# A Hyena and neighbourhood-attention layer: the order of the two tiles of each convolution product

## The chip, the cores and the metric

The kernel runs on one core of a Trainium2 chip. A core has a matrix engine (TensorE, PE in the profile; its weight loads are listed as PEld), a vector engine (VectorE, DVE), a scalar engine (ScalarE, ACT), a general engine (GpSimd, POOL) and a queue that only issues transfers here (SyncE, SP). Each works through its own list of instructions in order; semaphores make one wait for another. Matrix products go to PSUM, eight banks of 128 x 512 float32, and are copied from there to SBUF. The metric is the device time of one execution in microseconds; lower is better.

## The reference

One layer for two groups of tokens that share weights: 128 context tokens and 512 latent tokens, 640 columns together, 1024 channels. The input is modulated and projected; one branch is a gated long convolution, the other an attention; both are gated, projected, merged and normalised. What matters here is the convolution branch:

```python
hy, g_h, qkv, g_a, m = split(z)                      # z = h @ w_in
hy = short_conv(hy, conv_w, conv_b)                  # three taps along the sequence
v_h, x1, x0 = jnp.split(hy, 3, axis=-1)
...
u = v_h * x1
uf = jnp.fft.rfft(u, n=2 * L, axis=1)
ff = jnp.fft.rfft(filt_full, n=2 * L, axis=0)
y = jnp.fft.irfft(uf * ff, n=2 * L, axis=1)[:, :L]
y_h = (y + u * d_bias) * x0
...
p_h = (y_h * silu(g_h)) @ w_bh
```

So each channel of `u` is a product of two projected and three-tap-filtered values, `v_h` and `x1`. The order in which the two are made has no part in the result.

## The kernel before

Channels lie on the 128 partitions, tokens on the free axis (640 columns; 641 with a gap column between the two groups). A weight tile `wall[i]` gives 128 output channels. `proj(i)` (the loop of `accumulate`, L168) multiplies it in float32 split into a high and a low part: three passes (high x high, high x low, low x high) for each of 8 blocks of the inner dimension, in two halves of 320 columns, so 48 matmuls for each tile, into two PSUM banks of the pool `mm` (four banks, so two tiles). The split of the weights is made by ScalarE and VectorE (`split`, L101, L102), or, in the convolution part, by ScalarE (`wl` L147, `wh` L149) and an accumulating transfer that POOL issues (L148). `wh` has two buffers, `wl` three; the raw weights are loaded by SP (L63).

`conv_tile(i, dst)` runs `proj(i)`, copies the banks with four ScalarE instructions (L468 to L472) into one of two staging tiles `zs` in turn, and makes the three taps into `dst`: one on ScalarE (L474), two on VectorE (L476). Both `zs` and `dst` have to be free for that.

The 1024 channels of the convolution are done in four quarters of two tiles each, with these stages:

- `quarter_head(q)`: for each of the quarter's two tiles n the tile `u` (from `v_h`, weight tile n) and the tile `x1` (weight tile 8 + n), then `u = u * x1` (L499). `u` comes from a pool of four buffers (tag "u", each one row of tokens for 128 channels), so the tile of quarter q + 2 takes the buffer of quarter q; `x1` from a pool of two (tag "cv"), which `x0` shares.
- `long_conv(q)` and `long_conv_back(q)`: transposes (L531), the transform by matrix products (L156 to L158), the product with the filter's spectrum, the transform back (yb), transposes back (yp L616, y L626); then `u` takes the result in place (L619, L628) and is multiplied into the gated row `yh` (`gapped_product`, L457, L461), which goes to memory (L508). With that the buffer of `u` is free.
- `filter_spectrum(q)`: the spectrum of the filter, from small matmuls (fl, fa, fb, fc, fd, fp).
- `quarter_tail(q)`: `x0` (weight tile 16 + n) and the gate (24 + n, L481, L486), multiplied into `yh`.

The first quarter's head runs with its filter; then for q = 0, 1, 2 one generator chains the head of q + 1 and the tail of q, and another the transform of q and its way back with the filter of q + 1; `weave` interleaves the two by steps. That is the order in which the instructions are written. The order in which they stand on the engines is chosen by a scheduler that plays them through with a cost model and takes from each engine's candidates what is ready; PSUM banks and buffers are dealt out as it goes. A change of the written order so moves other instructions too. The fourth quarter's transform runs with the first steps of the attention. When it is done, the memory of the convolution is released to the attention's tiles: POOL clears the mask tiles (L792), the mask is loaded, and keys are copied out (`k_half`, L712, L717).

After the attention, a merge stage multiplies the rows `yh` by `w_bh` (L168, L481), with the gate's rows added on VectorE (L1189), then the attention's rows by `w_ba`; an output projection and the normalisation end the kernel.

Of the kernel before, what the change touches and what calls it, by code (L numbers as in the profile page):

```python
# [45 lines left out]
def tile_hyena_natten_step(ctx: ExitStack, tc: tile.TileContext, a, o):  # L46
# [126 lines left out]
    def proj(i, xh=None, xl=None, eng=None):  # L173
        if i in banks:
            return banks.pop(i)
        w = wtile(i, eng)
        ps = bank(i)
        for k in range(NK):
            accumulate(ps, w, k, xh[k] if xh else hH[:, k], xl[k] if xl else hL[:, k])
            if k < NK - 1:  # L180
                yield
        return ps
# [267 lines left out]
    def by_row(t):  # L450
        return t.rearrange("p (r b c) -> p r b c", r=8, b=8)

    def from_blocks(t, n):
        return t.rearrange("p (b r c) -> p r b c", b=n, r=8)
# [8 lines left out]
    def conv_tile(i, dst):  # L463
        lo, hi = yield from proj(i, eng="dma")
        convw = out["convw"]
        zs = zss[0]
        zss.reverse()
        nc.scalar.activation(zs[:, 1 : 1 + LP], lo[:, :LP], AF.Copy)  # L468
        nat = by_row(zs[:, GAP + 1 : NG + 1])
        nc.scalar.activation(nat[:, :, 7:8], from_blocks(lo[:, B7], 1), AF.Copy)  # L470
        nc.scalar.activation(nat[:, :, 0:2], from_blocks(lo[:, B01], 2), AF.Copy)  # L471
        nc.scalar.activation(nat[:, :, 2:7], from_blocks(hi[:, :HALF], 5), AF.Copy)  # L472
        d = dst[:, :NG]
        nc.scalar.activation(d, zs[:, 1 : 1 + NG], AF.Identity, scale=convw[:, i, 1:2], bias=convw[:, i, 3:4])  # L474
        for c in (0, 2):
            nc.vector.scalar_tensor_tensor(d, zs[:, c : c + NG], convw[:, i, c : c + 1], d, op0=ALU.mult, op1=ALU.add)  # L476
# [12 lines left out]
    def quarter_head(q):  # L489
        us = []  # L490
        out[f"u{q}"] = us
        for i in range(2):
            n = 2 * q + i
            u = hw.tile([P, NG + 1], F32, tag="u", bufs=4, name=f"u{n}")
            x1 = hwa.tile([P, NG + 1], F32, tag="cv", bufs=2, name=f"x1_{n}")
            yield from conv_tile(n, u)
            yield
            yield from conv_tile(8 + n, x1)
            nc.vector.tensor_tensor(u[:, :NG], u[:, :NG], x1[:, :NG], op=ALU.mult)  # L499
            us.append(u)  # L500
            yield
# [147 lines left out]
    with tc.manual_schedule(engines={mybir.EngineType.PE, mybir.EngineType.DVE, mybir.EngineType.Activation}):  # L649
        prologue()  # L650
    tc.keep_in_program_order(last[0])
    head = quarter_head(0)
    next(head)
    dft_consts()
    weave(head, filter_spectrum(0), 2 + NK, N_FILTER)
    pinned[0] = False
    for q in range(3):
        weave(chain(quarter_head(q + 1), quarter_tail(q)), chain(long_conv(q), braid(long_conv_back(q), filter_spectrum(q + 1))),
              8 * NK, N_CONV + N_BACK + N_FILTER)
# [799 lines left out]
```

## Time and profile before

| | |
|---|---|
| median of 3 runs | 905.71 us (902.41 to 907.54) |
| profiled execution | 906.42 us, span 904.4 us, mean granted clock 0.993 |
| PE, PEld busy | 881.4 us (97%), 850.8 us (94%) |
| DVE, ACT, POOL busy | 625.2 us (69%), 423.9 us (47%), 162.4 us (18%) |
| moved by transfers | 124.43 MB, mean 138 GB/s |

A line of the profile names the source line (L168), the engine, the operation, and the tiles as output <- input with buffer numbers left out; so all `conv_tile` products are `mm`. "x672" counts instructions. Behind a bar or in brackets stands the idle time of the engine just before, with what ended it. In a table by stretches, each row gives the stretch, its length, then busy time and number of instructions of PE, PEld, DVE, ACT and POOL, the granted clock of TensorE as a share of full speed, the share of the transfer engines and GB/s. A list of waits gives the total in us, how often, and the longest.

Times of instructions of a kind overlap: a matmul's listed length (about 0.31 us for 320 columns) is longer than the distance from one start to the next, so distances are what counts for TensorE.

### The profile page before, as it was taken

The numbers are of one execution on the slowest core, as the hardware profiler recorded it, in microseconds if no ns is written. First come the engines' busy times: TensorE is split into PE (matmuls) and PEld (weight loads), VectorE is DVE, ScalarE is ACT, GpSimd is POOL, SyncE is SP. The second block draws the span as 40 slices with busy tenths as digits, with TensorE's granted clock in tenths as the row PEclk, the third lists the DMA queues.
The fourth block names the chain that finished last, engine by engine and source line by source line (L and its number), as shares of the span: only waits on it lengthen the run. The fifth ranks groups of instructions, "written<-read, shape, count | busy, mean of one in ns | idle before, by whom it ended". The sixth has DMA issues, their size and how long they took to land. (4 is left out here: it accounts for less than half of the span.)

```text
span 904.4 us, 16943 instructions
## 1 busy us (share of the span) xinstructions
PE 881.4 (97%) x6560; PEld 850.8 (94%) x6560; DVE 625.2 (69%) x1229; ACT 423.9 (47%) x909; POOL 162.4 (18%) x188
## 2 busy tenths in 40 slices
PE   8999999999999999999999999899999999999994
PEld 7899999999999999999999999899999989999883
DVE  4776784794777678488867578756767567567665
ACT  4395455645455333265566455545655532233200
POOL 0011010101001000086653322332332000000000
PEclk9999999999999999999999999999999999999997
DMA  8965655665646222323233322332343677445322
GB/s 310 400 166 135 137 133 119 153 127 127 154 101 151 75 62 92 108 83 88 78 110 119 117 80 90 113 120 89 119 132 100 187 279 234 168 163 181 121 96 87
DMA packets 56715, 124.43 MB, mean 138 GB/s; under 512 B 8603, under 2 KB 28059, under 8 KB 56636
## 3 DMA queue, kind: packets, MB, share of 16 engines
q1 hardware_dynamic: 46988, 103.07, 35.2%
q0 software_dynamic: 4032, 14.68, 10.0%
q10 hardware_dynamic: 5616, 5.61, 1.8%
q8 instruction: 52, 0.85, 0.4%
q14 instruction: 27, 0.22, 0.1%
HBM read 109.18 MB, written 14.16 MB: 136 GB/s over the span
## 5 line engine op out<-in xcount | busy, mean ns | idle before, releaser
L168 PE MATMUL mm<-hH,wh 128*128 128x320 f32 x672 | 160.1, 312 | 1.8 <-ACT zs L471 1.0
L168 PE MATMUL mm<-hH,wl 128*128 128x320 f32 x672 | 158.4, 310 | 0.4 <-DVE wl L102 0.4
L168 PE MATMUL mm<-hL,wh 128*128 128x320 f32 x672 | 158.6, 311 | 0.0
L168 PEld LDWEIGHTS mm<-hH,wh 128*128 128x128 f32 x672 | 112.9, 188 | 4.7 <-issue 1.8
L168 PEld LDWEIGHTS mm<-hH,wl 128*128 128x128 f32 x672 | 113.5, 188 | 1.3 <-DVE wl L102 0.9
L168 PEld LDWEIGHTS mm<-hL,wh 128*128 128x128 f32 x672 | 113.3, 188 | 1.1 <-DVE hL L315 0.5
L1054 PE MATMUL sp<-t,wb 128*128 128x320 f32 x672 | 105.4, 310 | 0.0
L1054 PEld LDWEIGHTS sp<-t,wb 128*128 128x128 f32 x672 | 99.5, 188 | 0.3 <-issue 0.3
L1054 PE MATMUL sp<-hH,wb 128*128 128x320 f32 x336 | 82.1, 314 | 0.5 <-DVE c L1069 0.5
L101 ACT ACTIVATE wh<-raw 128x1024 fp32r<-128x1024 f32 x38 | 40.2, 1061 | 70.3 <-PE mm L168 40.3
L148 POOL DMA_DIRECT2D wl<-wall x28 | 24.4, 871 | 262.6 <-ACT wl L147 225.0
L102 DVE TENSOR_TENSOR wl<-raw,wh 128x1024 fp32r<-128x1024 f32 x38 | 47.2, 1245 | 26.1 <-ACT wh L101 25.9
L1054 PEld LDWEIGHTS sp<-hH,wb 128*128 128x128 f32 x336 | 57.9, 188 | 2.8 <-issue 1.7
L149 ACT ACTIVATE wh<-raw 128x1024 fp32r<-128x1024 f32 x28 | 29.7, 1060 | 52.7 <-PE mm L168 52.6
L101 ACT ACTIVATE wb<-s 128x512 fp32r<-128x512 f32 x56 | 34.8, 628 | 41.8 <-DVE s L1027 28.7
L102 DVE TENSOR_TENSOR wb<-s,wb 128x512 fp32r<-128x512 f32 x56 | 39.1, 705 | 19.9 <-ACT wb L101 19.6
L1054 PE MATMUL sp<-hL,wb 128*128 128x320 f32 x168 | 51.8, 309 | 0.0
L168 PE MATMUL mm<-yhs,wh 128*128 128x320 f32 x256 | 49.6, 314 | 1.5 <-DVE mh L481 1.5
L840 POOL TENSOR_SCALAR p<-p,sm 128x384 f32<-128x384 f32 x32 | 45.1, 1421 | 25.2 <-DVE sm L839 13.9
L1283 PE MATMUL out<-woh,yhs 128*128 128x512 f32 (+1 forms) x176 | 45.6, 373 | 0.0
L168 PEld LDWEIGHTS mm<-yhs,wh 128*128 128x128 f32 x256 | 41.3, 192 | 1.8 <-issue 1.7
L840 POOL TENSOR_SCALAR edge<-edge,sm 128x320 f32<-128x320 f32 x32 | 42.4, 1337 | 2.8 <-DVE sm L839 2.8
(352 smaller groups left out, 2012.2 us busy)
## 6 DMA issues: line engine op xcount, KB each, us to landing
raw<-wall SPq DMA_DIRECT2D x96, 512.0 KB, 3.7
wl<-wall POOLq DMA_DIRECT2D x28, 512.0 KB, 5.7
ada<-wada SPq DMA_DIRECT2D x16, 512.0 KB, 8.0
gate<-wgate SPq DMA_DIRECT2D x8, 512.0 KB, 6.6
wo<-wall SPq DMA_DIRECT2D x8, 512.0 KB, 4.4
xt<-xT SPq DMA_DIRECT2D x8, 320.0 KB, 8.0
dec<-decay SPq DMA_DIRECT2D x20, 128.0 KB, 3.1
yh_d<-yh SPq DMA_DIRECT2D x8, 320.0 KB, 2.5
```

What stands on the lines that cost most here:

```text
L101: hi = nc.scalar.activation(dst_h, src, AF.Copy)
L102: return hi, (eng or nc.vector).tensor_tensor(dst_l, src, f(dst_h), op=ALU.subtract)
L148: nc.gpsimd.dma_start(wl, a["wall"][i], accum_op=ALU.add)
L149: nc.scalar.activation(wh, raw[:], AF.Copy)
L168: nc.tensor.matmul(ps[hf][:, :HALF], wt[k], x[:, hf * HALF : (hf + 1) * HALF], start=(i == 0 and k == 0), stop=(i == lead[2] and k == NK - ...
L840: nc.gpsimd.tensor_scalar_mul(pv, pv, sm[:, 2:3])
L1054: nc.tensor.matmul(dst, wk, x(xi, k), start=j < 4 and k == 0 and i == 0, stop=k == 3 and i == 2, skip_group_check=True,)
L1283: ins = nc.tensor.matmul(dst, m[k][:, c0 : c0 + P], w[:, c : c + n], start=(first and k == 0), stop=(last and k == 5), skip_group_check=True,)
```

## The change

In the first quarter's head nothing changes: `u`, then `x1`. In the heads of the second, third and fourth quarters `x1` is made first and `u` second. The buffers are asked for in the same order as before, `u` ahead of `x1`, the product stays behind both, and the step at which the generator hands over between the two tiles stays between them.

```diff
@@ quarter_head(q)
             n = 2 * q + i
             u = hw.tile([P, NG + 1], F32, tag="u", bufs=4, name=f"u{n}")
             x1 = hwa.tile([P, NG + 1], F32, tag="cv", bufs=2, name=f"x1_{n}")
-            yield from conv_tile(n, u)
-            yield
-            yield from conv_tile(8 + n, x1)
+            tiles = ((n, u), (8 + n, x1))
+            for i_, dst in tiles if q == 0 else tiles[::-1]:
+                yield from conv_tile(i_, dst)
+                if i_ == tiles[q > 0][0]:
+                    yield
             nc.vector.tensor_tensor(u[:, :NG], u[:, :NG], x1[:, :NG], op=ALU.mult)
             us.append(u)
             yield
```

## The prediction

> **What bounds the kernel now.** First the page's head, then busy time in stretches of 20 us, to see where TensorE is not the bound.
>
> ```profile
> span 904.4 us, 16943 instructions
> PE 881.4 (97%) x6560; PEld 850.8 (94%) x6560; DVE 625.2 (69%) x1229; ACT 423.9 (47%) x909; POOL 162.4 (18%) x188
> ```
>
> ```profile
> 0.00:20.00 20.00, 17.29 (x140) 13.65 (x141) 8.60 (x19) 9.10 (x14) 0.99 (x13) 1.00 0.82 297
> ...
> 220.00:240.00 20.00, 19.82 (x140) 19.32 (x139) 12.11 (x23) 8.77 (x15) 1.73 (x2) 1.00 0.62 145
> 240.00:260.00 20.00, 18.97 (x137) 18.78 (x138) 13.68 (x22) 12.01 (x28) 1.73 (x2) 1.00 0.54 113
> ...
> 560.00:580.00 20.00, 17.15 (x128) 16.23 (x127) 14.19 (x39) 10.45 (x31) 8.46 (x8) 1.00 0.42 122
> ...
> 720.00:740.00 20.00, 17.92 (x112) 17.38 (x111) 12.53 (x16) 6.55 (x8) 0.00 (x0) 0.91 0.75 266
> ...
> 760.00:780.00 20.00, 20.00 (x138) 20.00 (x137) 15.74 (x20) 5.61 (x7) 0.00 (x0) 1.00 0.63 214
> ...
> 880.00:900.00 20.00, 11.57 (x74) 10.27 (x72) 13.19 (x29) 0.86 (x3) 0.00 (x0) 0.86 0.30 99
> ```
>
> The second column is TensorE's busy time. It is full nearly everywhere; the holes are the start, the end, and four spots. The convolution part, which the change touches, runs from about 50 to 380 us, and its only holes are those of 220 to 260: 20.00 - 19.82 = 0.18 and 20.00 - 18.97 = 1.03 us. The list of what TensorE waited for names them:
>
> ```profile
> PE pt L856 <- ACT ptsp L948: 3.0, 2, 2.4
> ...
> PE mm L168 <- DVE mh L481: 1.5, 1, 1.5
> PE mm L168 <- ACT zs L471: 1.0, 1, 1.0
> ...
> PE fp L156 <- DVE w3s L372: 0.2, 1, 0.2
> ```
>
> So what the change can win on TensorE in its own stage is 1.03 + 0.18 = 1.21 us. The time order shows how the 1.03 arises (start, length, engine; in brackets the idle time before):
>
> ```profile
> 232.37 2.21 DVE L628 SCALAR_TENSOR_TENSOR u<-u,hyd,y 128x512 f32<-128x512 f32 x2 [1.97 <-PE y L626]
> 234.51 0.74 DVE L461 TENSOR_TENSOR yh<-yh,u 128x64 f32<-128x64 f32 x2
> ```
>
> ```profile
> 235.29 0.93 ACT L474 ACTIVATE u<-zs,pack 128x641 f32<-128x641 f32 x1 [3.69 <-DVE yh L461]
> ...
> 239.84 0.39 PE L156 MATMUL fp<-sh,dftH 128*128 128x256 f32 x1 [0.18 <-DVE w3s L372]
> ...
> 240.31 0.87 DVE L476 SCALAR_TENSOR_TENSOR u<-zs,pack,u 128x641 f32<-128x641 f32 x1
> 240.63 0.26 ACT L468 ACTIVATE zs<-mm 128x128 f32<-128x128 f32 x1
> ...
> 241.42 0.28 ACT L471 ACTIVATE zs<-mm 128x128 f32<-128x128 f32 x1
> ...
> 241.75 0.42 PE L168 MATMUL mm<-hH,wh 128*128 128x320 f32 x1 [1.03 <-ACT zs L471]
> ```
>
> This is the head of the fourth quarter: u6, x1_6, u7, x1_7, then x0_4. u6 takes the slot of u2, which the inverse transform of an earlier quarter still needs: its last reader is the pair of L461 at 234.51. ScalarE stands 3.69 us at L474. Until the last L476 of u6 at 240.31 + 0.87 = 241.18, the staging tile zs of u6 is not free, so u7, which uses the same zs, can't be taken out of its PSUM banks; x1_7 is taken out at 240.63, late behind the blocked ScalarE, and x0_4 can't begin before 241.75.
>
> **The change, part by part.** No instruction is added or removed: the same tiles, 48 matmuls each, in the order x1, u, x1, u. The order of the two built programs differs only from the end of the third quarter's head on (for the second quarter, names are swapped, and u2 and u3 have fresh slots: nothing). Moved with the tiles are their weight loads on SP and the accumulating ones on POOL. Both queues keep their lengths; SP swaps some neighbours (a decay load and a write of yh against a weight load), POOL one pair of mask additions much later. The rows of 220 to 260 show 145 and 113 GB/s, far below the 266 of 720 to 740: taken as zero, between -0.2 and +0.5 us.
>
> *Third quarter (u4, u5).* TensorE shows no wait there, so nothing can be won. In the new order L474 of u4 stands ahead of a weight conversion that in the old one waited for TensorE anyway. Zero, between -0.2 and +0.5 us.
>
> *Fourth quarter.* Now x1_6 is first, u6 second, x1_7 third, u7 fourth. x1_6 frees its zs at once, so x1_7 leaves PSUM freely and x0_4 takes its banks without a wait: -1.03. What is late next? The scheduler also put the transposes that L628 waits for 14 matmuls further back (28 of the u7 tile stand before them, where 14 of x1_7 did). A matmul of this kind starts every 20.00 / 138 = 0.145 us (the row 760 to 780), so L628 starts 14 x 0.145 = 2.0 us later, at about 234.4. From the start of L628 to the last L476 VectorE does the same list as before: 241.18 - 232.37 = 8.8 us, so it ends at 243.2. ScalarE reaches L474 as early as before and still waits there, some 3 to 4 us: the wait stays, what is lost to it changes. u7 leaves PSUM by 243.2 + (241.42 + 0.28 - 240.63) = 244.3. Its banks are wanted after x0_4: fp's start without its wait 239.66, + 48 x 0.145 = 7.0 for x0_4, + some 1.4 for the ten small matmuls between = 248.1. Cover: 3.8 us. Only if VectorE is later than that does a wait return. The 0.18 before fp goes too, since fp now stands 38 matmuls (5.5 us) further back. Sum here: -1.21 us; bounds -1.21 (all gone) and +2.0 (the delay of L628 paid in full and nothing won).
>
> *End of the convolution.* The moved work pushes the fourth quarter's inverse transform back: its last transposes stand behind 38 matmuls of v where 12 stood. The rows that touch this (time order, 374 to 406):
>
> ```profile
> 377.36 0.64 PE L748 MATMUL v<-wh,hH 128*128 128x256 f32 x4
> 377.84 0.64 PE L748 MATMUL v<-wh,hL 128*128 128x256 f32 x4
> ...
> 388.88 0.46 PE L168 MATMUL mm<-hH,wh 128*128 128x320 f32 x2
> ...
> 389.47 0.46 PE L168 MATMUL mm<-hH,wl 128*128 128x320 f32 x2
> ...
> 405.40 0.52 PE L856 MATMUL pt<-pack,p 128*128 128x128 f32 x3 [0.65 <-ACT ptsp L948]
> ```
>
> ```profile
> 380.35 1.81 POOL L792 MEMSET tm<- 128x128 f32 x12 [91.79 <-DVE yh L461]
> ...
> 394.83 1.20 POOL L891 TENSOR_SCALAR pp<-pp,smp 128x128 f32<-128x128 f32 x2 [0.62 <-DVE smp L889]
> 397.38 4.12 POOL L840 TENSOR_SCALAR edge<-edge,sm 128x320 f32<-128x320 f32 x2 [1.35 <-DVE sm L839]
> 401.48 2.75 POOL L840 TENSOR_SCALAR p<-p,sm 128x384 f32<-128x384 f32 x2
> ```
>
> ```profile
> 380.18 0.56 ACT L712 ACTIVATE k<-mm 128x64 fp32r<-128x64 f32 x3 [5.77 <-DVE yh L461]
> ...
> 385.12 1.06 ACT L101 ACTIVATE wh<-raw 128x1024 fp32r<-128x1024 f32 x1 [3.51 <-PE ve L760]
> ```
>
> ```profile
> 386.21 1.60 DVE L102 TENSOR_TENSOR wl<-raw,wh 128x1024 fp32r<-128x1024 f32 x1 [3.77 <-ACT wh L101]
> ```
>
> A matmul of v starts every (377.84 - 377.36) / 4 = 0.12 us, so the release of the convolution's memory comes 26 x 0.12 = 3.1 us later against TensorE. Two things hang on it. ScalarE's L712 goes from 380.2 to 383.3 on TensorE's clock; with its 0.56 and the like for VectorE's copy behind it the bank is free at some 384.5. The next to want it is ve, which now begins 24 x 0.12 = 2.9 us ahead of 388.88, at 386.0: covered by 1.5. POOL's mask work moves by 3.1 and has 0.62 + 1.35 = 2.0 us of idle time to take it up; 1.1 us is left over. Its p at 401.48 ends at 404.23, and its second half is used at 405.40, which leaves 1.2: just covered. Zero, between -0.7 (the 0.65 at 405.40 gone) and +3.1.
>
> In the same place the 24 matmuls of ve now stand in one piece ahead of the gate tile of 388.88; before, twelve stood far earlier. The conversion of that tile's weights waits for the first twelve (the idle time of 3.51 at 385.12). From their end: 12 x 0.12 = 1.44 us until the gate tile, 4 x 0.145 = 0.58 more until its first use of wl, so 2.0; the conversion takes 1.06, and wl 1.22 to 1.60 behind it, so 2.3 to 2.7. A new wait of 0.3 to 0.7; I take 0.5.
>
> Sum: -1.21 + 0.5 = -0.7 us. Against the profiled execution's own 906.42 (span 904.4) that is 905.7; this execution lies 0.71 above the median of the runs shown, 905.71, so I say 905.0.
>
> **What a stall costs beyond itself.** Stretches of 2 us around the two longest stalls (TensorE's busy time second, the granted clock third from last):
>
> ```profile
> 730.00:732.00 2.00, 1.61 (x11) 1.35 (x10) 0.84 (x2) 1.06 (x1) 0.00 (x0) 1.00 1.00 370
> 732.00:734.00 2.00, 0.87 (x4) 0.60 (x4) 2.00 (x4) 1.15 (x2) 0.00 (x0) 1.00 0.66 263
> 734.00:736.00 2.00, 1.44 (x5) 1.44 (x6) 2.00 (x4) 0.64 (x1) 0.00 (x0) 0.54 0.17 39
> 736.00:738.00 2.00, 2.00 (x10) 2.00 (x10) 2.00 (x3) 0.00 (x0) 0.00 (x0) 0.61 0.85 339
> ...
> 566.00:568.00 2.00, 0.43 (x4) 0.46 (x5) 1.57 (x4) 2.00 (x6) 2.00 (x2) 1.00 0.42 137
> 568.00:570.00 2.00, 2.00 (x16) 2.00 (x16) 0.52 (x2) 0.95 (x3) 1.48 (x2) 1.00 0.90 237
> ```
>
> The idle time of 2.08 us between 730 and 736 is followed by a granted clock of 0.54 and 0.61, which costs up to 2.00 x 0.46 + 2.00 x 0.39 = 1.7 us more; the single one of 2.4 us near 566 (the longest wait for ptsp above) is followed by none. So a new stall of two microseconds may cost 3.7, or 2. [...]
>
> **The rivals.**
> - *The wait returns elsewhere, no gain.* The third and fourth quarters' VectorE is crowded, and a later L628 pushes all behind it. For it: L474 keeps its wait. Against it: the 3.8 us of cover. From there on each microsecond costs one; with the fourth quarter's bound of +2.0 and the 0.5 of ve, 906.42 + 2.5 = 908.9. Within 0.5%.
> - *Slower: the late release of the convolution's memory decides.* POOL is delayed by 3.1 us at the start of attention. For it: POOL's p ends at 404.23, 1.2 us before its use. Against it: POOL's 2.0 us of idle time. It begins to count when more than 3.2 us of delay arrive; if nothing is absorbed, 3.1 are paid, 0.5 for ve and 1.7 for a clock that falls: 906.42 - 1.21 + 3.1 + 0.5 + 1.7 = 910.5, on the edge of 0.5%; if VectorE's delay of 2.0 comes on top, 912.5.
> - *Faster: the stall at 732 goes.* It hangs on when loads land in a stage whose order is nearly the same, but which starts at another moment. It is 2.08 + 1.7 = 3.8 us long: 906.42 - 1.21 + 0.5 - 3.8 = 901.9, just under 0.5%. For it: the runs shown reach from 902.41 to 907.54, so something of that size does come and go. Against it: VectorE's order there is one swap away from the old, and later.
> - *The change does nothing* (the wait costs TensorE as much as before): 906.42 + 0.5 = 906.9.
>
> **How the numbers follow.** Half a per cent, 4.5 us, is about what a measurement of this kernel tells from no change, since the runs shown spread over 907.54 - 902.41 = 5.1 us. Forecast (a change of -2.5 to +1 us): 0.52. Wait returned or nothing won (+1 to +4.5): 0.22. Slower by more: 0.13. Stall at 732 gone: 0.13, about two thirds of it past 0.5%, the more so as other stalls may shrink with it; with some weight for gains that no row shows I put faster at 0.12. Slower by over 0.5% 0.13, within 0.75. The range reaches from the faster rival's 901.9, less 0.9 for the spread, to just under the slower one's 910.5: 901.0 to 909.8. The forecast's own range is 903.2 to 906.7.
>
> **What would show it.** Right: the wait of TensorE for L471 near 241 gone; L474 still waiting for L461, some 3 to 4 us, but in front of a later tile; u7 out of PSUM about 4 us before its banks are wanted; POOL's first memset some 2 us later than 380.35, as TensorE is 1.2 ahead; a wait of 0.3 to 0.7 us for L102 at the gate tile of 388; the stalls of 566 and 732 as they were. Wrong: a wait of TensorE in the fourth quarter for L468 to L472; one of over 1 us between 385 and 410 for POOL or VectorE; a granted clock under 1.00 before 730; or a difference that lies only in the merge stage.

## The result, and the profile after

The changed kernel takes 907.90 us (median of 22 runs, 903.50 to 911.04), the kernel before 904.61 us (22 runs, 901.68 to 907.94). The ratio is 1.0028, 95% interval 1.0016 to 1.0040: slower by a little, where 0.7 us of gain had been forecast. The profiled execution of the changed kernel took 907.52 us, its span 905.4 us. In `quarter_head` the change added two lines, so all line numbers behind it are two higher in its profile (L833 is L835, L840 L842, L856 L858); runs listed below with the old numbers are written on the old lines.

The head of the page of the changed kernel, and the stretches that answer to those shown of before (TensorE's busy time second, VectorE, ScalarE and GpSimd fourth to sixth, the granted clock third from last):

```profile
span 905.4 us, 16942 instructions
PE 882.0 (97%) x6560; PEld 851.0 (94%) x6560; DVE 626.0 (69%) x1229; ACT 424.1 (47%) x909; POOL 163.7 (18%) x188
```

```profile
220.00:240.00 20.00, 20.00 (x146) 19.81 (x145) 10.04 (x19) 8.74 (x17) 1.73 (x2) 1.00 0.61 136
240.00:260.00 20.00, 20.00 (x145) 20.00 (x145) 13.58 (x23) 12.72 (x27) 1.73 (x2) 1.00 0.56 122
380.00:400.00 20.00, 19.74 (x155) 18.64 (x155) 15.51 (x38) 10.85 (x28) 15.19 (x28) 1.00 0.49 152
400.00:420.00 20.00, 17.30 (x112) 16.29 (x111) 12.14 (x29) 9.55 (x27) 16.87 (x16) 0.91 0.26 74
560.00:580.00 20.00, 16.97 (x118) 16.49 (x117) 13.64 (x36) 11.14 (x29) 9.21 (x9) 1.00 0.42 127
720.00:740.00 20.00, 19.23 (x130) 18.72 (x129) 12.39 (x17) 7.68 (x11) 0.00 (x0) 1.00 0.82 269
```

The fourth quarter's 1.21 us are won: TensorE is full from 220 to 260. A new hole of 0.26 us stands at 388, and a big one between 400 and 420: 20.00 - 17.30 = 2.70 us, with a clock of 0.91 beside it. Two marks in time order tell how much this is. The transposes of the prompt's probabilities (ptp) occur once per pair of heads; first before, then after, the first and the second of them:

```profile
403.38 0.38 PE L946 MATMUL ptp<-pack,pp 128*128 128x128 f32 x2
439.66 0.38 PE L946 MATMUL ptp<-pack,pp 128*128 128x128 f32 x2
```

```profile
402.55 0.38 PE L948 MATMUL ptp<-pack,pp 128*128 128x128 f32 x2
442.86 0.38 PE L948 MATMUL ptp<-pack,pp 128*128 128x128 f32 x2
```

At the first mark the changed kernel is 403.38 - 402.55 = 0.83 us ahead. At the second it is 442.86 - 439.66 = 3.20 us behind. So 4.03 us are lost in between, at the start of attention, and no loss of that size stands anywhere else.

What happens there: the scores of two blocks, for two heads each, lie in four auxiliary PSUM banks. VectorE reads them with the mask added (L833), ScalarE takes the exponential, GpSimd scales by the reciprocal sum (L891 for the prompt's pp, L840 for the others: "edge" in the first and last block, "p" in between), and TensorE transposes the result (L946, L856) into auxiliary banks that L833 has set free. TensorE's time order there in the changed kernel, VectorE's, and GpSimd's from its mask additions on:

```profile
402.83 0.55 PE L858 MATMUL pt<-pack,edge 128*128 128x128 f32 x3
404.97 0.52 PE L858 MATMUL pt<-pack,edge 128*128 128x128 f32 x3 [1.59 <-DVE sm L835]
405.73 0.55 PE L858 MATMUL pt<-pack,p 128*128 128x128 f32 x3 [0.24 <-POOL p L842]
407.14 0.90 PE L858 MATMUL pt<-pack,p 128*128 128x128 f32 x3 [0.87 <-POOL p L842]
```

```profile
402.29 1.21 DVE L102 TENSOR_TENSOR wl<-raw,wh 128x1024 fp32r<-128x1024 f32 x1
...
403.50 0.86 DVE L481 SCALAR_TENSOR_TENSOR sg<-sg,mm 128x320 f32<-128x320 f32 x2
...
404.35 0.47 DVE L835 CUSTOM_DVE_ANT_0 edge<-s,tm 128x320 f32<-128x320 f32 x1
```

```profile
386.07 0.60 POOL L809 TENSOR_TENSOR tm<-mask,tb 128x192 f32<-128x192 f32 x1 [2.11 <-DMA tb<-rpbT]
...
387.33 1.59 POOL L813 TENSOR_TENSOR tm<-mask,tb 128x192 f32<-128x192 f32 x1
388.88 1.58 POOL L809 TENSOR_TENSOR tm<-mask,tb 128x192 f32<-128x192 f32 x1
...
398.58 2.43 POOL L893 TENSOR_SCALAR pp<-pp,smp 128x128 f32<-128x128 f32 x2
400.99 3.46 POOL L842 TENSOR_SCALAR edge<-edge,sm 128x320 f32<-128x320 f32 x2
404.43 2.66 POOL L842 TENSOR_SCALAR p<-p,sm 128x384 f32<-128x384 f32 x2
```

Two things are late, one behind the other. VectorE reads the last scores only at 404.35, behind a weight conversion (L102, 1.21 us) and a gate (L481, 0.86); in the kernel before it read them first:

```profile
403.12 0.47 DVE L833 CUSTOM_DVE_ANT_0 edge<-s,tm 128x320 f32<-128x320 f32 x1
...
403.93 1.22 DVE L102 TENSOR_TENSOR wl<-raw,wh 128x1024 fp32r<-128x1024 f32 x1
405.06 0.87 DVE L481 SCALAR_TENSOR_TENSOR sg<-sg,mm 128x320 f32<-128x320 f32 x2
```

And GpSimd's p ends at 404.43 + 2.66 = 407.09, where it ended at 404.23. The 1.59 us are ended by the first, the 0.24 and 0.87 by the second. Behind the holes the clock falls (stretches of 2 us, columns as above):

```profile
402.00:404.00 2.00, 1.38 (x10) 1.00 (x9) 2.00 (x5) 1.11 (x3) 2.00 (x2) 1.00 0.13 37
404.00:406.00 2.00, 0.79 (x5) 0.58 (x6) 2.00 (x8) 1.14 (x4) 2.00 (x3) 1.00 0.00 0
406.00:408.00 2.00, 1.13 (x7) 0.90 (x6) 2.00 (x4) 1.47 (x5) 2.00 (x3) 0.72 0.05 8
408.00:410.00 2.00, 2.00 (x10) 2.00 (x9) 1.10 (x2) 1.11 (x2) 2.00 (x2) 0.50 0.60 96
410.00:412.00 2.00, 2.00 (x14) 2.00 (x14) 0.16 (x1) 0.45 (x1) 2.00 (x3) 0.92 0.59 231
```

That costs 2.00 x (0.28 + 0.50 + 0.08) = 1.72 us more. Sum between the marks: idle time 2.70 - 0.65 = 2.05, clock 1.72, together 3.77 of the 4.03.

The two profiled executions differ by 1.10 us only (907.52 and 906.42), mostly because the one of before had the stall at 732 with a fallen clock (2.08 + 1.70 us) and this one has 0.77 us and no fall there; that stall comes and goes. The medians differ by 3.29 us, about what the second mark shows. The mean granted clock over the 22 runs of the changed kernel is 0.9911, over the three groups of 29 to 31 runs of the kernel before that were taken with the experiments 0.9935 to 0.9944. By this estimate 0.0024 to 0.0033 of 905, or 2.2 to 3.0 us, go with the clock.

### The profile page after: what moved, and what is told of

Same layout as the page of the kernel before. It is cut to its first block, busy times and chain, and to the rows that moved or that the text cites. A ratio compares the mean times of both kernels' runs of the same rounds, so it can differ in the third digit from the quotient of the medians.

```text
span 905.4 us, 16942 instructions
## 1 busy us (share of the span) xinstructions
PE 882.0 (97%) x6560; PEld 851.0 (94%) x6560; DVE 626.0 (69%) x1229; ACT 424.1 (47%) x909; POOL 163.7 (18%) x188
## 5 line engine op out<-in xcount | busy, mean ns | idle before, releaser
L102 DVE TENSOR_TENSOR wl<-raw,wh 128x1024 fp32r<-128x1024 f32 x38 | 46.8, 1235 | 23.3 <-ACT wh L101 23.0
L102 DVE TENSOR_TENSOR wb<-s,wb 128x512 fp32r<-128x512 f32 x56 | 39.2, 707 | 19.5 <-ACT wb L101 19.4
L842 POOL TENSOR_SCALAR p<-p,sm 128x384 f32<-128x384 f32 x32 | 44.5, 1401 | 25.7 <-DVE sm L841 14.4
L842 POOL TENSOR_SCALAR edge<-edge,sm 128x320 f32<-128x320 f32 x32 | 41.4, 1304 | 1.4 <-DVE sm L841 1.4
```

The source lines that it names most:

```text
L102: return hi, (eng or nc.vector).tensor_tensor(dst_l, src, f(dst_h), op=ALU.subtract)
L842: nc.gpsimd.tensor_scalar_mul(pv, pv, sm[:, 2:3])
```

## The experiments

Theory A, from these rows: the fourth quarter's way back is late, so the convolution's memory is released late, and GpSimd's late work stalls TensorE at the start of attention. Rival B: the loss lies elsewhere in the new order. VectorE's part came up on the way, as theory D: VectorE is late there too, and either engine's lateness is enough for a stall. The table sums up what was measured; "idle" is TensorE's between 400 and 420, "clock" the granted one there, "mark" the start of the second ptp transposes, and the ratio is to the kernel before.

| | idle | clock | mark | ratio (95%) |
|---|---|---|---|---|
| before | 0.65 | 1.00 | 439.66 | |
| changed | 2.70 | 0.91 | 442.86 | 1.0028 (1.0016 to 1.0040) |
| e1 changed, GpSimd's additions moved | 1.12 | 1.00 | 439.33 | 1.0006 (0.9989 to 1.0024) |
| e2 before, the same | 0.09 | 1.00 | 438.97 | 0.9998 (0.9982 to 1.0014) |
| e3 before, GpSimd made late | 3.39 | 0.91 | 443.17 | 1.0052 (1.0030 to 1.0074) |
| e4 swap in the fourth quarter only | 1.58 | 1.00 | 439.72 | 1.0006 (0.9985 to 1.0027) |
| e5 changed, way back at its old place | 0.61 | 1.00 | 438.03 | 0.9980 (0.9965 to 0.9995) |
| e6 changed, e1 and edge scaled on ScalarE | 2.27 | 0.91 | 441.70 | 1.0029 (1.0015 to 1.0042) |
| e7 before, the same as e6 | 0.00 | 1.00 | 438.36 | 0.9984 (0.9972 to 0.9995) |
| e8 swap in second and third quarters only | 2.45 | 0.83 | 445.20 | 1.0049 (1.0036 to 1.0063) |
| e9 changed, VectorE's old order | 2.82 | 0.91 | 442.35 | 1.0026 (1.0006 to 1.0046) |
| e10 changed, e1 and e9 | 0.18 | 1.00 | 438.05 | 1.0007 (0.9990 to 1.0024) |
| e11 changed, e5 and e6 | 0.00 | 1.00 | 436.58 | 0.9981 (0.9963 to 0.9999) |
| e12 before, half the dose of e3 | 1.47 | 1.00 | 440.69 | 1.0077 (1.0048 to 1.0107) |

### GpSimd's part: e1, e2, e3, e12

e1 and e2 move five of GpSimd's mask additions behind the first scalings:

```diff
@@ bias_tile(hd): the second and third addition
-        nc.gpsimd.tensor_tensor(two(tm[:, 320:832])[:, :, :P], ...)
-        nc.gpsimd.tensor_tensor(tm[:, 832:], ...)
+        (tc.keep_in_program_order if hd in (2, 3) else whole)(nc.gpsimd.tensor_tensor(two(tm[:, 320:832])[:, :, :P], ...))
+        (tc.keep_in_program_order if hd in (2, 3) else whole)(nc.gpsimd.tensor_tensor(tm[:, 832:], ...))
```

> The changed kernel, with one thing moved on GpSimd alone: the five mask additions of heads 2 and 3, which stand ahead of the first scaling of the probabilities (L891, L840), are put behind the scaling of the first two tiles. TensorE's, VectorE's and ScalarE's lists stay as they are. Theory A (the late release makes GpSimd late at the start of attention): in the changed kernel these five took 0.74 + 0.60 + 1.14 + 1.31 + 1.18 = 4.97 us between 392.8 and 398.6; without them the scaling of pp begins some 4 us earlier, TensorE's idle time of 2.70 us between 400 and 420 falls under 0.8, the granted clock stays at 1.00 there, and what is left of the change is its gain of 1.21 less 0.26 at the gate tile: a ratio to the kernel before of 0.999 (0.9975 to 1.0005). Rival B (the loss lies elsewhere in the new order: the third quarter, the merge stage, the weight loads): the ratio stays at 1.002 to 1.004 although GpSimd is early.

> The kernel before, with the same move of the five mask additions on GpSimd. Both theories: TensorE has one wait there, 0.65 us at 405.40, so a gain of 0 to 0.7 us, ratio 0.9990 to 1.0005. It is the partner of the changed kernel with the same move: theory A says that the two then differ by 1.0 us (0.95 to 1.2, some 0.1%) in favour of the change; rival B that the changed one is still 2 to 4 us slower.

e3 makes each addition of heads 0 and 1 twice, e12 those of head 0:

```diff
@@ bias_tile(hd): each of the three additions
-        nc.gpsimd.tensor_tensor(...)
+        [nc.gpsimd.tensor_tensor(...) for _ in range(1 + (hd < 2))]
```

> The kernel before, without the swap, with GpSimd made late: the six mask additions of heads 0 and 1 are made twice (the result is the same). All lists of TensorE, VectorE and ScalarE stay as they are. The six took 0.60 + 0.73 + 0.59 + 0.59 + 1.72 + 0.59 = 4.8 us. Theory A: of 4.8 us, 2.0 go into GpSimd's idle time and 1.2 into the lead that p had, so 1.6 us or more of TensorE's waiting return between 400 and 412, with a granted clock under 1.00 behind it: ratio 1.0015 to 1.005, without any swap. Rival B: GpSimd's lateness is covered, ratio 0.9995 to 1.0008.

> The kernel before with half the dose: the three mask additions of head 0 are made twice (six were, in the run with GpSimd late: ratio 1.0052, idle 3.39 us). They take 0.60 + 0.73 + 0.59 = 1.9 us, or up to 4.5 beside VectorE. With 2.0 us of GpSimd's idle time and the 1.2 us lead of p: idle time of TensorE from 400 to 420 between 0.65 and 2.0 us, the clock at 1.00, ratio 1.000 to 1.002. If the granted clock falls at under 2 us of idle time here, 1.7 us more.

Without any swap, late work on GpSimd alone makes the kernel slower, 1.0052, with the waits that theory A names (list of waits of e3 between 385 and 425: total, times, longest):

```profile
PE pt L856 <- POOL p L840: 2.6, 2, 1.6
PE pt L856 <- POOL edge L840: 0.8, 1, 0.8
```

With GpSimd relieved (e1) the clock stays up and the mark is reached at 439.33, but 1.12 us of idle time are left where under 0.8 had been expected, and no gain in the time. The list of waits of e1 names what is left:

```profile
PE pt L856 <- DVE sm L833: 1.1, 1, 1.1
```

So theory A was too narrow. The additions moved also come back later: e1 and e2 wait 0.7 and 1.1 us for GpSimd's p just behind the second mark, where the kernel before waits 0.3. e12 is a miss: 1.000 to 1.002 was expected and 1.0077 measured. Its profile shows 1.47 us and no fall of the clock, as expected, but it was the fastest of only six runs (905.49 against a median of 909.70), and the six have a mean clock of 0.9923. Why half the dose is not less than the whole is open; the two intervals overlap. So e3 and e12 show the direction, not what a microsecond of GpSimd's lateness costs.

### The swap, or the place of the way back: e4, e8, e5

```diff
@@ quarter_head(q), e4 (e8 with q in (1, 2))
-            for i_, dst in tiles if q == 0 else tiles[::-1]:
+            for i_, dst in tiles[::-1] if q == 3 else tiles:
```

> The swap in the fourth quarter's head alone; second and third quarters in the old order. The last transposes of the way back stand 196 matmuls ahead of the first transposes of attention, as in the changed kernel (222 in the kernel before). Theory A: all that the change does is done by this: the 1.03 us wait at 241 is gone, GpSimd is late by the same amount, TensorE idles 2 to 3 us between 400 and 412, ratio 1.002 to 1.004. Rival B in the form that the third quarter's swap brings the loss: ratio 0.998 to 0.9995.

> The swap in the second and third quarters alone; the fourth keeps the old order, so the wait of 1.03 us at 241 should stay or change little. The scheduler nevertheless puts the last transposes of the way back 191 matmuls ahead of attention's first (222 in the kernel before, 196 in the changed one). Theory A: no gain, and GpSimd later than in the changed kernel: TensorE idles 2 to 4 us between 400 and 412, its clock falls, ratio 1.003 to 1.006. Rival C (the fourth quarter's swap itself costs, not the place of the way back): ratio 0.9995 to 1.0005.

e5 keeps the whole change and holds four matmul groups on TensorE behind parts of the way back (yb, yb, yb, y), which gives these their old distance from attention:

```diff
@@ proj, values: TensorE's issue order
+    AHEAD = {(33, 7): 'back3_0', (41, 4): 'back3_1', ('v1', 0): 'back3_2', ('v1', 1): 'back3_y'}
-            accumulate(ps, w, k, ...)
+            with held(i, k): accumulate(ps, w, k, ...)     # issue after the transform named for (tile, block)
```

> The changed kernel, whole, with the fourth quarter's way back put at its old place on TensorE: its last transposes (L626) stand 222 matmuls ahead of the first transposes of attention as in the kernel before, where the changed kernel has 196; GpSimd's list stays. Theory A: the memory is released 26 x 0.12 = 3.1 us earlier against TensorE, GpSimd's scaling of p ends at 404 or before, TensorE's idle time of 400 to 420 is under 1 us, its clock stays 1.00, and the gain of the fourth quarter is kept: ratio 0.999 (0.9975 to 1.0005), TensorE at the second transposes of the prompt's probabilities at 438.5 to 439.0 (kernel before 439.66, changed kernel 442.86). Rival B (the place of the way back is not what costs): ratio 1.002 to 1.004 and 442 to 443.

e5 is the clearest of the runs. With the way back at its old place the whole change is a gain, 0.9980, its interval under 1. The mark comes at 438.03, half a microsecond ahead of the 438.5 to 439.0 expected. That rules out rival B, which expected 1.002 to 1.004 here. One edit, and both late things are gone: GpSimd's eleven mask additions ahead of pp take 9.38 us (9.29 before, 11.96 in the changed kernel), and VectorE's list at the start of attention is the old one again, with the read of the scores ahead of the conversion (time order of e5):

```profile
401.49 0.47 DVE L833 CUSTOM_DVE_ANT_0 edge<-s,tm 128x320 f32<-128x320 f32 x1
...
402.30 1.21 DVE L102 TENSOR_TENSOR wl<-raw,wh 128x1024 fp32r<-128x1024 f32 x1
```

e8 is the reverse: no swap in the fourth quarter, so no gain there (1.30 us of idle time from 220 to 260, 1.21 before), but a way back 31 matmuls later, and 1.0049. In its row the clock is 0.83, from a fall that costs 3.40 us where the others cost 1.70 to 1.72:

```profile
400.00:420.00 20.00, 17.55 (x101) 16.30 (x100) 13.22 (x29) 8.62 (x23) 18.43 (x17) 0.83 0.27 77
```

So it isn't the fourth quarter's swap that costs (rival C of e8): the late place comes with either set of heads. e4 has the late place and VectorE's new order, but misses its expectation of 2 to 3 us and 1.002 to 1.004: it waits 1.58 us, all for VectorE's read, and keeps its clock: 1.0006, between. Its interval holds 1.000 and 1.002, so it decides little beside the profile.

### VectorE's part: e6, e7, e9, e10

e6 and e7 take two of GpSimd's scalings away on top of e1 and e2:

```diff
@@ probs(j, b, s, tm)
-            nc.gpsimd.tensor_scalar_mul(pv, pv, sm[:, 2:3])
+            nc.scalar.activation(pv, pv, AF.Copy, scale=sm[:, 2:3]) if j == b == 0 else nc.gpsimd.tensor_scalar_mul(pv, pv, sm[:, 2:3])
```

> The changed kernel with GpSimd relieved twice: the five mask additions of heads 2 and 3 behind the first scalings, and the two scalings of the first edge tiles (3.46 us on GpSimd) on ScalarE. TensorE's and VectorE's lists stay. Theory A: TensorE waits for nothing between 400 and 412 (the changed kernel 2.70 us, with the additions alone moved 1.12), clock 1.00; against the kernel before it has the 1.21 - 0.26 of the fourth quarter and its 0.65 near 405 besides: ratio 0.998 (0.9965 to 0.9995), second transposes of the prompt's probabilities at 437.7 to 438.5. Rival B: no better than with the additions alone, ratio 1.000 or more.

> The kernel before with the same two edits of GpSimd's work. Theory A: no wait between 400 and 412, 0.65 us won, ratio 0.9993 (0.998 to 1.0005), second transposes of the prompt's probabilities at 438.7 to 439.2: 0.95 us behind the changed kernel with the same edits, which is what the swap is worth once GpSimd is out of the way. Rival B: the two are alike or the changed one is slower.

e7 came out a little better than expected (mark 438.36 for 438.7 to 439.2); e6 is the miss that overthrew theory A as the whole cause. GpSimd has its p ready at 395.81 + 4.40 = 400.21, before TensorE gets there, and TensorE waits all the same (time order of GpSimd, then the waits between 385 and 425, both of e6):

```profile
395.81 4.40 POOL L840 TENSOR_SCALAR p<-p,sm 128x384 f32<-128x384 f32 x2 [1.47 <-DVE sm L839]
```

```profile
PE pt L856 <- DVE sm L833: 2.3, 1, 2.3
PE mm L168 <- DVE wl L102: 0.7, 1, 0.7
```

The wait for VectorE is even longer than in e1 (1.1): two of VectorE's instructions ahead of the read, which fall beside the moved additions here, take 1.44 and 1.61 us where e1 has 0.79 and 1.21 (time order of e6):

```profile
400.71 1.44 DVE L725 TENSOR_TENSOR kl<-ck,k 128x128 fp32r<-128x128 f32 x2
402.07 1.61 DVE L102 TENSOR_TENSOR wl<-raw,wh 128x1024 fp32r<-128x1024 f32 x1
```

Theory D: VectorE's late read keeps the bank that the second transposes need, and GpSimd's late scaling keeps the data of the last; either is enough for a stall. e9 takes away the first alone, e10 both:

```diff
@@ wtile, gate_tile: VectorE's issue order ("read" is the L833 of edge31 in the first pair of heads)
-                split(wh, wl, raw[:, n * j : n * j + n], eng)
+                with tc.issue_after(out["read"].ins) if i == T_K + 2 else nullcontext(): split(...)
-            gate(dst[:, cs], p)
+            with tc.issue_after(out["read"].ins) if i == T_GA + 1 else nullcontext(): gate(dst[:, cs], p)
```

> The changed kernel with VectorE's old order at the start of attention only: the conversion wl42 (L102) and the gate of sg1 (L481) stand behind the read of the last scores (L833, edge30 and edge31), as in the kernel before; the changed kernel has them ahead. TensorE's list stays, GpSimd's but for one addition. Theory D (two waits, one behind the other: VectorE's late read of the scores holds the PSUM bank of the second transposes, and GpSimd's late p holds the last): the 1.59 us for L833 goes, and since GpSimd's second p still ends near 407 TensorE waits for that instead: idle time of 400 to 420 still 2.0 to 2.8 us (2.70 in the changed kernel), ratio 1.001 to 1.003. If VectorE's order alone were the cause: idle under 0.7, ratio 0.998 to 1.000. If GpSimd alone: 2.7, ratio 1.003.

> The changed kernel with VectorE's old order as in the run beside it and GpSimd's five additions behind the first scalings. Theory D: both waits gone, idle time of TensorE from 400 to 420 under 0.7 us (1.12 with GpSimd's alone moved), clock 1.00, second transposes of the prompt's probabilities at 438.2 to 438.9, ratio 0.9985 (0.997 to 1.000). If there is a third wait: idle time over 1 us.

The waits of e9, then of e10, between 385 and 425:

```profile
PE pt L856 <- POOL p L840: 2.3, 2, 1.6
PE pt L856 <- DVE sg L481: 0.5, 1, 0.5
```

```profile
PE mm L168 <- DVE wl L102: 0.3, 1, 0.3
PE pt L856 <- ACT ptsp L948: 0.2, 1, 0.2
```

Theory D holds. With VectorE alone mended, the wait passes to GpSimd and the time stays (2.82 us, 1.0026); with GpSimd alone mended, VectorE's is left (1.12 and 2.27 in e1 and e6); with both, 0.18 us. The mark of e10 is 439.66 - 438.05 = 1.6 us ahead of the kernel before, a little more than expected. Its time isn't shorter: 1.0007. About half of the 1.6 us goes into a wait behind the mark that is 0.31 us in the kernel before (TensorE's time order of e10):

```profile
441.05 0.52 PE L856 MATMUL pt<-pack,p 128*128 128x128 f32 x3 [1.14 <-POOL p L840]
```

The moved additions bring it in a roundabout way. Between 398 and 420 SyncE stands 14.6 us in all for the last addition of a head (L811; 4.4 us in the kernel before), whose buffers the next table loads need. The weight load behind these is late, ScalarE's conversion waits for it, and VectorE's reads and GpSimd's p come behind that (time order of ScalarE in e10; in the kernel before, the idle time at this place is 3.57 us and not put down to a load):

```profile
414.73 1.06 ACT L101 ACTIVATE wh<-raw 128x1024 fp32r<-128x1024 f32 x1 [5.53 <-DMA raw<-wall]
```

What is left of the gain, some 0.6 us, is too small to show in an interval of 0.9990 to 1.0024.

### All together: e11

> The changed kernel with the way back at its old place on TensorE, the five additions behind the first scalings and the first edge tiles scaled on ScalarE. With the way back early TensorE had 0.61 us of idle time left between 400 and 420; all three edits together should leave none. Theory D: ratio 0.9975 (0.996 to 0.999), second transposes of the prompt's probabilities at 437.4 to 437.9, some 0.6 us ahead of the run with the way back alone.

The edits are those of e5 and e6. TensorE waits for nothing between 400 and 420, and behind the mark only the wait of 0.28 us is left that the kernel before has there too (0.31):

```profile
400.00:420.00 20.00, 20.00 (x162) 19.38 (x162) 16.10 (x42) 10.81 (x34) 17.29 (x17) 1.00 0.35 113
420.00:440.00 20.00, 19.72 (x161) 18.94 (x160) 19.90 (x46) 13.60 (x35) 15.45 (x13) 1.00 0.18 50
```

Its mark, 436.58, is the earliest of all, 3.1 us ahead of before (2.2 of it already at the first mark, 401.15, which is more than the edits explain and in part chance), and its median, 901.18 us against 903.90, the lowest of all kernels here; its ratio, 0.9981, can't be told from that of e5 or e7.

## Why the prediction was wrong

*Right.* The fourth quarter: both waits gone, -1.21 us; ScalarE still waits at L474 (forecast 3 to 4 us, measured 4.64) but in front of a later tile, and the tile u7 leaves its banks from 243.97 to 244.88 (forecast: all out by 244.3), 3.2 us before the next tile starts at 248.07 (forecast 248.1, with 3.8 us of cover):

```profile
237.99 0.93 ACT L474 ACTIVATE u<-zs,pack 128x641 f32<-128x641 f32 x1 [4.64 <-DVE yh L461]
...
243.97 0.28 ACT L468 ACTIVATE zs<-mm 128x128 f32<-128x128 f32 x1 [0.82 <-DVE u L476]
...
244.41 0.47 ACT L472 ACTIVATE zs<-mm 128x320 f32<-128x320 f32 x1
```

```profile
248.07 0.46 PE L168 MATMUL mm<-hH,wh 128*128 128x320 f32 x2
```

The third quarter and the queues cost nothing. The wait at the gate tile of 388 came, mis-sized: 0.26 us for 0.5 (0.3 to 0.7). Up to 403 the sum is thus -0.95 by the rows, and the mark shows -0.83.

*The step that failed* is the last of the sum but one, the end of the convolution: the release 3.1 us later against TensorE, "just covered", taken as zero. In its place stand the 3.77 us from above: 2.05 of idle time and 1.72 of a fallen clock. The release did come late, GpSimd's first memset at 381.79 for 380.35, which is 1.44 us by the clock (forecast some 2) and 2.3 against TensorE, and GpSimd's cover was worked out from durations of before. But those did not hold. GpSimd's eleven mask additions ahead of pp took 9.29 us before and 11.96 us after: three of them 1.18 to 1.72 us before and seven 1.14 to 1.59 us after, all ten beside an instruction of VectorE, the others 0.59 to 0.75. The first, third and fourth of them before, to be read against the rows of 386.07, 387.33 and 388.88 after:

```profile
384.33 0.60 POOL L807 TENSOR_TENSOR tm<-mask,tb 128x192 f32<-128x192 f32 x1 [1.81 <-DMA tb<-rpbT]
...
385.59 0.59 POOL L811 TENSOR_TENSOR tm<-mask,tb 128x192 f32<-128x192 f32 x1
386.14 0.59 POOL L807 TENSOR_TENSOR tm<-mask,tb 128x192 f32<-128x192 f32 x1
```

That alone is 2.7 us, where the step had 0.1 us of cover left: 1.2 of lead, less the 1.1 of delay that GpSimd's idle time of 2.0 did not take up. So p ended 407.09 - 404.23 = 2.86 us later by the clock and some 3.7 later against TensorE, not 1.1.

*What the step left out* is that the scheduler's order changes far behind the moved tiles as well. The prediction followed TensorE's order through and took the other engines' lists at the start of attention as they were. There VectorE's conversion and gate had gone ahead of the read of the last scores, some 160 us behind the fourth quarter's head. VectorE's list in the built program is where this could have been read; the prediction drew on that list for the fourth quarter and the merge stage, not for the start of attention.

*The rivals.* The one that came is "slower: the late release of the convolution's memory decides", in its place and with its fallen clock (1.7 us forecast, 1.72 measured); it was given 0.13. Its price, 910.5 - 906.42 = 4.1 us, was 0.8 too high against the medians' 3.29, and 1.3 against the 2.8 of the rows: the idle time came to 2.05 for 3.1, the gate tile's wait to 0.26 for 0.5. Its condition, that more than 3.2 us of delay reach GpSimd's p, was met by slower additions, which it didn't name, and VectorE's order was in none of the rivals. The measured 907.90 lies in the whole range, 901.0 to 909.8, and outside the forecast's own, 903.2 to 906.7. That the time lies inside the whole range is owed to this rival, not to the mechanism forecast: the forecast was 0.7 us of gain. Of what should show it wrong, the wait of over 1 us between 385 and 410 came true (1.59 us for VectorE; 1.11 for GpSimd, in two pieces), and so did a granted clock under 1.00 before 730.

*The clock.* Of the two stalls that the prediction weighs, that of 730 to 738 was the nearer: 2.08 us of idle time had a fall behind them there, and 2.70 here. With the fall the change comes to -1.21 + 0.26 + 2.05 + 1.72 = +2.8 us by the rows; without it, it would be +1.1.

## What to carry to other kernels

When a scheduler orders the engines, a swap of two tiles can reorder any engine's list anywhere behind it; compare every engine's order to the end of the stage in which the moved buffers are released, not only the one that was edited. A wait with two late causes doesn't yield to either cure: mend both, or the thing that makes both late, which here was one place in TensorE's order (0.9980 for the change with that place held). And a cover worked out from durations did not hold here when the neighbours moved: the same addition on GpSimd took up to 2.7 times as long beside VectorE's work (1.59 us after, 0.59 before).

## What the runs showed of the hardware

*The clock's falls.* In the fourteen profiles there are thirteen falls of TensorE's granted clock between 100 and 860 us: twelve cost 1.70 to 1.72 us each by the sum of 2.00 x (1 - clock) over the stretches, one 3.40 (e8, behind 2.45 us of idle time). No idle time of 1.61 us or less (added up over neighbouring stretches) had a fall behind it; all three over 2.6 us had one (2.70 in the changed kernel, 2.81 in e9, 3.40 in e3); of the twenty from 1.72 to 2.59 us ten had one and ten not, with no order by length: 1.72 us had one (e9), 2.59 us none (e11). What decides between the two no run here shows.

*GpSimd beside VectorE.* In the changed kernel an addition of 192 columns took 0.60 us at 386.07, with VectorE idle, and 1.59 and 1.58 us at 387.33 and 388.88, beside conversions of VectorE (L102) that took 1.23 us at 387.24 and 1.32 at 388.68. In the kernel before a conversion took 1.60 us at 386.21, beside additions of 0.59 and 1.72 us, and 1.22 us at 403.93, beside one of 1.39. No run here took the two engines apart, so what lengthens these instructions is not shown.
